# First attention of a hybrid encoder layer: three groups of key blocks per unit, the short rests stacked, ten transposes instead of twelve

## The chip, the cores and the metric

The kernel runs on one core of a Trainium2 chip. TensorE (PE) multiplies matrices and writes to PSUM; VectorE (DVE) and ScalarE (ACT) take results out of PSUM; GpSimd (POOL) works between SBUF tiles; SyncE (SP) issues most transfers. The metric is the time of one execution in device microseconds, as the median of three runs.

## The reference

One layer of an encoder on 2048 tokens of 1024 features: a norm, a projection to queries, keys, values and gates, two attentions, a gated merge, and a feed-forward part of 4096 features. All inputs are float32. The first attention is the one that is changed:

```python
def windowed_gqa(q, k, v, sink):          # 8 query heads, 2 key heads, 64 features each
    def block(i):                         # 128 queries, 384 keys: the block and its two neighbours
        qi = qb[:, i]
        ki = lax.dynamic_slice_in_dim(kp, i * A_BLOCK, 3 * A_BLOCK, axis=1)
        vi = lax.dynamic_slice_in_dim(vp, i * A_BLOCK, 3 * A_BLOCK, axis=1)
        dist = jnp.abs(q_pos[:, None] - k_pos[None, :])
        valid = (dist <= A_WINDOW) & (k_pos[None, :] >= 0) & (k_pos[None, :] < s)
        sc = jnp.einsum('bqkgd,bskd->bkgqs', qi, ki).astype(jnp.float32) * scale
        sc = sc - slopes[:, :, None, None] * dist.astype(jnp.float32)
        sc = jnp.where(valid, sc, -jnp.inf)
        p = jax.nn.softmax(jnp.concatenate([sc, sink_col], axis=-1), axis=-1)[..., :-1]
        return jnp.einsum('bkgqs,bskd->bqkgd', p.astype(v.dtype), vi)
```

A query sees the keys at most 128 tokens away, so of the 384 keys of a block each query uses 257.

## The kernel before, in words

Dense products are made of split operands: a value is written as a rounded high part and a low part (the rest), and products of both are added in PSUM. `hl` tiles hold the two parts of weights, `ph` and `pl` the two parts of attention weights, and a tile of v holds its high part in 64 columns and its low part in 64 more, so that one product with v gives two sums of 64 rows each, which L813 and L814 add.

The work runs in stages: the projections by a fast matrix scheme (`zb`), then the first attention (`attn_a`), the second attention (`attn_b`), the merge, and the feed-forward part (`b`). While the attentions run, pieces of the remaining projections are put in as filler (`mm`, lines 203 to 205); `paced` holds each piece back until the attention unit of a given number has issued its last product.

A unit of the first attention is one key head g and one block i of 128 queries with its four query heads; there are 32 units, 28 with three blocks of keys and four (i = 0 and i = 15, for each g) with two. Inside a unit the queries are arranged as four sub-blocks u of 32 queries by four heads, so that each u has 128 rows, and sub-block u needs only the 288 keys from 32u to 32u + 287 of the 384. In order:

- L770 to L774: q is loaded (`qraw`, SP) and brought into the order of sub-blocks on POOL (`qa`).
- L784, L786: for each u, two products give the scores of 288 keys (PE), and DVE adds the bias and takes the maximum into `s`, a tile of 128 rows by 4 by 384.
- L788 to L793: ACT makes the exponentials and their sums, DVE the reciprocal `ri`.
- L795: POOL multiplies each u by its reciprocal, the shares.
- L802 to L808, for each block c of 128 keys: four transposes into a PSUM bank `pt`, ACT copies it to `ph`, DVE makes `pl`, and two products of 512 columns with v add to `po` (`av`).
- L813, L814: the two halves of `po` are added into `ya`, which SP stores.

Columns of `s` outside a sub-block's 288 keys are zero from the start (L753), so they add nothing to the product.

`drive` starts a unit (up to the shares) two units ahead of the one whose transposes and products are being issued. The order of instructions on each engine is not written out: a planner simulates the program with its own durations and orders each engine's queue by that; the chip then keeps each queue in order. Tiles are taken from pools that grow from the left and the right end of SBUF; a tile that lies where another one lay waits for the last use of that one. The left pools of the first attention are, in order, ka1, va1, qraw, qa, sta, sa, ya, ph, pl, biasa1 and byhead; the second attention's pools (masks, kb0, qb0, braw0, biass0, stb, biass1, qb1, ...) come from the right while the first attention's last units still run. The second attention's biases (`biass0`, `biass1`, `biasl`) are built on POOL at L915, its scores are products at L947 with maxima at L952, its shares are made at L963, its transposes at L975, its splits at L980 and L981, its products at L987.

Of the kernel before, what the change touches and what calls it, by code (L numbers as in the profile page):

```python
# [22 lines left out]
P = 128  # L23
# [72 lines left out]
def encoder_layer(ctx, tc, x, norm_mix, w_in, b_gate, sink, rpb, w_pa, w_pb, w_out,  # L96
# [12 lines left out]
    def pools(stack, side, tags, name):  # L109

        return {t: pool(f"{name}_{t}", side=side, stack=stack) for t in tags}
# [9 lines left out]
    def psum(tag, bufs):  # L121
        n_ps[0] += 1
        return pps[tag].tile([P, 512], F32, tag=tag, bufs=bufs, name=f"{tag}_{n_ps[0]}")
# [549 lines left out]
    s_a = ExitStack()  # L673
    ap_ = pools(s_a, "left", ("ka1", "va1", "qraw", "qa", "sta", "sa", "ya", "ph", "pl", "biasa1", "byhead"), "a")
    ap_.update(pools(s_a, "right", ("biasa0", "va0", "ka0"), "a"))
# [79 lines left out]
    def load_kv(g, m, behind=None):  # L755
        k, kd = kas[g][:, :, m * (S // 2) : (m + 1) * (S // 2)], ks_a[m][g]
        with tc.issue_after(behind) if behind else nullcontext():
# [3 lines left out]
            SY.dma_start(vas[g][:, 8 * m : 8 * m + 8].bitcast(F32), vs_a[m][g])  # L761

    def attn_a(g, i):
        c0, c1 = (1 if i == 0 else 0), (2 if i == 15 else 3)
# [8 lines left out]
        began.append(SY.dma_start(by_head, qs_a[g][i // 8][:, :, i % 8]).ins)  # L773
        G.tensor_copy(out=q.rearrange("p u h q -> p h u q"), in_=by_head.rearrange("p h (u q) -> p h u q", u=4))  # L774
        ka, v = kas[g], vas[g]
        st = T(ap_, [P, 8, 4], F32, "sta", 8)
# [15 lines left out]
        V.tensor_tensor(out=sm, in0=sm, in1=es, op=ALU.add)  # L792
        V.reciprocal(ri, sm)  # L793
        for u, (lo, hi) in enumerate(span):
            share = G.tensor_scalar(s[:, u, lo:hi], s[:, u, lo:hi], ri[:, u : u + 1], 1.0, ALU.mult, ALU.mult)  # L795
        shares.append(share.ins)
        yield
        po = psum("av", 1)
        for c in range(c0, c1):
            pt = psum("pt", 2)  # L800
            for u in range(4):
                PE.transpose(pt[:, u * P : (u + 1) * P], s[:, u, c * P : (c + 1) * P], ident)  # L802
            ph = T(ap_, [P, 512], F32R, "ph", 3)
            pl = T(ap_, [P, 512], F32R, "pl", 3)
            A.copy(ph, pt)
            V.tensor_tensor(out=pl, in0=pt, in1=ph.bitcast(F32), op=ALU.subtract)
            PE.matmul(po, v[:, i - 1 + c, :], ph, start=c == c0, stop=False)
            last = PE.matmul(po, v[:, i - 1 + c, :], pl, start=False, stop=c == c1 - 1).ins  # L808
        done.append(last)
# [846 lines left out]
```

## Time and profile before

| | |
|---|---|
| Time, median of 3 runs (lowest to highest) | 2607.2 us (2606.03 to 2607.28) |
| The profiled execution | 2605.6 us, span 2603.8 us |
| PE, weight loads, DVE, ACT, POOL busy | 2571.4, 2143.3, 1608.0, 1232.4, 368.1 us |
| Instructions | 34627 |

All times of the profile are from the start of the span of the profiled execution. A row of a group of instructions reads: line of the kernel, engine, operation, output from inputs by the names of the tiles, shapes as partitions by elements, count, busy time in us, mean ns of one, and the idle time of the engine just before them with what ended it. A row of the timeline reads: start, length, engine, line, operation and tiles, count of merged instructions, and in brackets the idle time before it. `PEld` is the loading of weights into TensorE, which overlaps its products. The ends of products are modelled; their starts are not.

### The profile page before, as it was taken

To read this page: it belongs to the slowest core of one execution; us is meant where nothing else is said; L and a number is where in the kernel's file an instruction comes from. 1 tells how busy PE (TensorE), PEld (TensorE's weight loads), DVE (VectorE), ACT (ScalarE), POOL (GpSimd) and SP (SyncE) were. 2 spreads that over 40 slices of the span, in tenths; PEclk is the share of its full clock that TensorE was granted. 3 is DMA by queue.
4 is the path that set the end of the run, shared out by engine and by line. 5 is a ranking of instruction groups with operands and counts; after the bars stand their busy time and mean duration, and the time that the engine had idled before them with its cause. 6 is when DMAs were issued, how large, how long until landed. Compare 5 with 4: busy or idle time off the path is not lost.

```text
span 2603.8 us, 34627 instructions
## 1 busy us (share of the span) xinstructions
PE 2571.4 (99%) x12140; PEld 2143.3 (82%) x12140; DVE 1608.0 (62%) x2621; ACT 1232.4 (47%) x2261; POOL 368.1 (14%) x493
## 2 busy tenths in 40 slices
PE   8999999999999999999999999999999999999999
PEld 6888788788888888888888888888888888888887
DVE  8865666665544444665478677766656535554766
ACT  5334356666555555542335544644444322323454
POOL 1000124444655541000000000100000000000010
PEclk9999999999999999999999999999999999999999
DMA  5657486465975745865466665854428825445555
GB/s 185 203 155 202 132 260 166 119 167 154 247 212 173 207 140 188 273 202 161 143 198 207 238 222 200 306 173 146 158 100 313 290 97 186 146 148 167 186 193 171
DMA packets 354127, 490.40 MB, mean 188 GB/s; under 512 B 28808, under 2 KB 188808, under 8 KB 351776
## 3 DMA queue, kind: packets, MB, share of 16 engines
q1 hardware_dynamic: 346896, 471.14, 57.6%
q10 hardware_dynamic: 7056, 17.04, 1.8%
q8 instruction: 96, 1.57, 0.2%
q14 instruction: 79, 0.65, 0.1%
HBM read 328.64 MB, written 159.45 MB: 187 GB/s over the span
## 4 chain that ended last, share of the span: by engine, by line
PE 90%; DVE 4%; DMA 2%; ACT 2%; issue 1%; SPq 0%; POOL 0%; DVEq 0%; POOLq 0%; ACTq 0%
PE b L300 15%; PE b L302 15%; PE b L301 15%; PE mm L203 6%; PE mm L205 6%; PE mm L204 6%; PE zb L300 3%; PE zb L302 3%; PE zb L301 3%; PE pt L203 2%; PE pt L204 2%; PE pt L205 2%; PE av L987 2%; PE pt L975 2%; PE s L947 2%; PE pt L802 1%
## 5 line engine op out<-in xcount | busy, mean ns | idle before, releaser
L301 PE MATMUL b<-dwh,dah 128*128 128x512 f32 x896 | 348.5, 389 | 0.0
L302 PE MATMUL b<-dwh,dah 128*128 128x512 f32 x896 | 347.6, 389 | 0.0
L300 PE MATMUL b<-dwh,dah 128*128 128x512 f32 x896 | 339.6, 389 | 0.0
L296 ACT CAST dah<-da 128x1024 fp32r<-128x1024 f32 (+1 forms) x128 | 120.9, 945 | 368.0 <-PE b L302 245.9
L297 DVE TENSOR_TENSOR dah<-da,dah 128x1024 fp32r<-128x1024 f32 (+1 forms) x128 | 139.5, 1090 | 221.3 <-ACT dah L296 216.8
L301 PE MATMUL b<-ubh,uwhlb 128*128 128x512 f32 x592 | 230.3, 389 | 0.0
L300 PE MATMUL b<-ubh,uwhlb 128*128 128x512 f32 x592 | 230.2, 389 | 0.0
L302 PE MATMUL b<-ubh,uwhlb 128*128 128x512 f32 x592 | 229.2, 389 | 0.0
L203 PE MATMUL mm<-hT,whl 128*128 128x512 f32 x544 | 218.6, 402 | 0.0
L205 PE MATMUL mm<-hT,whl 128*128 128x512 f32 x544 | 215.2, 396 | 0.0
L204 PE MATMUL mm<-hT,whl 128*128 128x512 f32 x544 | 214.4, 394 | 0.0
L301 PEld LDWEIGHTS b<-dwh,dah 128*128 128x128 f32 x896 | 168.2, 188 | 35.0
L302 PEld LDWEIGHTS b<-dwh,dah 128*128 128x128 f32 x896 | 168.2, 188 | 34.9
L300 PEld LDWEIGHTS b<-dwh,dah 128*128 128x128 f32 x896 | 168.2, 188 | 34.9
L300 PE MATMUL zb<-zh,zwhl 128*128 128x512 f32 x476 | 186.7, 394 | 8.3 <-DVE zc L293 3.5
L301 PE MATMUL zb<-zh,zwhl 128*128 128x512 f32 x476 | 186.5, 392 | 0.0
L302 PE MATMUL zb<-zh,zwhl 128*128 128x512 f32 x476 | 183.5, 392 | 0.3 <-DVE zwhl L297 0.3
L293 DVE TENSOR_TENSOR uc<-b,uc 128x512 f32<-128x512 f32 x160 | 109.1, 689 | 105.0 <-PE b L302 104.0
L1526 POOL TENSOR_TENSOR st<-st,power 128x1 f32<-128x1 f32 x16 | 13.4, 841 | 925.2 <-DVE st L1525 925.2
L300 PEld LDWEIGHTS b<-ubh,uwhlb 128*128 128x128 f32 x592 | 111.1, 188 | 23.4 <-issue 0.4
L301 PEld LDWEIGHTS b<-ubh,uwhlb 128*128 128x128 f32 x592 | 111.1, 188 | 23.2
L302 PEld LDWEIGHTS b<-ubh,uwhlb 128*128 128x128 f32 x592 | 111.1, 188 | 23.1
(254 smaller groups left out, 5839.3 us busy)
## 6 DMA issues: line engine op xcount, KB each, us to landing
at<-uc SPq DMA_DIRECT2D x224, 256.0 KB
da<-at SPq DMA_DIRECT2D x96, 512.0 KB
dw<-in_w_down_dram SPq DMA_DIRECT2D x160, 256.0 KB
uraw<-in_w_up_dram SPq DMA_DIRECT2D x32, 1024.0 KB
raw<-in_w_in_dram SPq DMA_DIRECT2D x34, 512.0 KB
zraw<-in_w_in_dram SPq DMA_DIRECT2D x16, 1024.0 KB
z<-zg SPq DMA_DIRECT2D x64, 256.0 KB
qraw<-qs_a SPq DMA_DIRECT2D x32, 256.0 KB
```

The costliest lines, as they stand in the source:

```text
L203: PE.matmul(ps, lh, rh, start=first, stop=False)
L204: PE.matmul(ps, lh, rl, start=False, stop=False)
L205: PE.matmul(ps, ll, rh, start=False, stop=last)
L293: return eng.tensor_tensor(out=out, in0=a, in1=b, op=op).ins
L296: A.copy(hi, src)
L297: return eng.tensor_tensor(out=lo, in0=src, in1=hi.bitcast(F32), op=ALU.subtract).ins
L300: PE.matmul(ps, lh, rh, start=first, stop=False, skip_group_check=True)
L301: PE.matmul(ps, lh, rl, start=False, stop=False, skip_group_check=True)
L302: PE.matmul(ps, ll, rh, start=False, stop=last, skip_group_check=True)
L947: PE.matmul(ps[:, :n], q[:, i, :], kv[:, z, B_R0[i] // 4 : (B_R0[i] + B_NR[i]) // 4, 4 * B_C0[j] : 4 * (B_C0[j] + w)], start=z == 0, stop= ...
L975: PE.transpose(pt[:kp, at + (i - i0) * P : at + (i - i0 + 1) * P], s[i][:, rr : rr + kp], ident)
L987: last = PE.matmul(po[:, i0 * P : (i0 + ni) * P], v[:kp, c, :], src[:kp, o : o + ni * P], start=first, stop=(c == 7 and z == 1), skip_grou ...
```

## The change

A unit's transposes, splits and products are put in three groups instead of one per block of keys.

- The first group is block 1, which all four sub-blocks use in full: four transposes, `ph` and `pl`, two products of 512 columns.
- The second is block 0 for u = 0 and 1 and block 2 for u = 2 and 3: four transposes into one bank, one `ph` and one `pl`, and for each of the two blocks two products of 256 columns.
- The third holds the rests: block 2 for u = 0 and 1 (32 and 64 keys) and block 0 for u = 2 and 3 (64 and 32 keys). The rest of u = 1 is put beside that of u = 0, in columns 320 to 383 of u = 0, and that of u = 3 beside that of u = 2, in columns 32 to 63 of u = 2. So one transpose brings two rests, and two transposes do for the group. In `ph` the high part of each rest takes 64 rows and its low part the other 64, written by DVE to the other half of the partitions; one product of 256 columns for each block, with a tile `ve` that holds the 64 rows of v twice, gives both.

DVE writes the moved rests scaled by the reciprocal; POOL's shares leave those columns out. The doubled rows of v are copied on POOL, four copies of 64 rows by 128 columns per unit (two in an edge unit), into a new pool `ve` of three buffers of 1 KB, at the end of the left pools. All products of a unit are listed in `todo` and issued behind its transposes and splits. An inner unit has 10 transposes, two products of 512 columns and six of 256; an edge unit 7, two and three.

```diff
--- before.py
+++ after.py
@@ -671,7 +671,7 @@
     s_h = ExitStack()
     hpl = [pool(f"hT{n}", side="left", stack=s_h) for n in range(4)]
     s_a = ExitStack()
-    ap_ = pools(s_a, "left", ("ka1", "va1", "qraw", "qa", "sta", "sa", "ya", "ph", "pl", "biasa1", "byhead"), "a")
+    ap_ = pools(s_a, "left", ("ka1", "va1", "qraw", "qa", "sta", "sa", "ya", "ph", "pl", "biasa1", "byhead", "ve"), "a")
     ap_.update(pools(s_a, "right", ("biasa0", "va0", "ka0"), "a"))
     hp = {}
 
@@ -760,6 +760,9 @@
             SY.dma_start(k[64:128, 1].bitcast(F32), kd[0:64])
             SY.dma_start(vas[g][:, 8 * m : 8 * m + 8].bitcast(F32), vs_a[m][g])
 
+    def v_rows(g, k, c):
+        return vas[g][64 - 32 * c : 128 - 32 * c, k]
+
     def attn_a(g, i):
         c0, c1 = (1 if i == 0 else 0), (2 if i == 15 else 3)
         if bias_a[g] is None:
@@ -772,6 +775,12 @@
         s = sas[len(began) % 4]
         began.append(SY.dma_start(by_head, qs_a[g][i // 8][:, :, i % 8]).ins)
         G.tensor_copy(out=q.rearrange("p u h q -> p h u q"), in_=by_head.rearrange("p h (u q) -> p h u q", u=4))
+        ve = T(ap_, [P, 2, P], F32R, "ve", 3)
+        for c in (0, 2):
+            if c0 <= c < c1:
+                rows = v_rows(g, i - 1 + c, c)
+                for half in (slice(0, 64), slice(64, P)):
+                    G.tensor_copy(out=ve[half, c // 2], in_=rows)
         ka, v = kas[g], vas[g]
         st = T(ap_, [P, 8, 4], F32, "sta", 8)
         mx, nm, sm, es, ri = (st[:, k, :] for k in range(5))
@@ -791,21 +800,53 @@
             A.activation(s[:, u, lo:hi], s[:, u, lo:hi], AF.Exp, bias=nm[:, u : u + 1], accum_out=sm[:, u : u + 1])
         V.tensor_tensor(out=sm, in0=sm, in1=es, op=ALU.add)
         V.reciprocal(ri, sm)
+        for u, lo, hi, at in ((1, 2 * P, span[1][1], s[:, 0, 320:384]), (3, span[3][0], P, s[:, 2, 32:64])):
+            if lo < hi:
+                V.tensor_scalar(at, s[:, u, lo:hi], ri[:, u : u + 1], 1.0, ALU.mult, ALU.mult)
         for u, (lo, hi) in enumerate(span):
+            lo, hi = max(lo, P if u == 3 else 0), min(hi, 2 * P if u == 1 else hi)
             share = G.tensor_scalar(s[:, u, lo:hi], s[:, u, lo:hi], ri[:, u : u + 1], 1.0, ALU.mult, ALU.mult)
         shares.append(share.ins)
         yield
         po = psum("av", 1)
-        for c in range(c0, c1):
+        todo = []
+
+        def whole(keys):
             pt = psum("pt", 2)
-            for u in range(4):
+            for u, c in keys:
                 PE.transpose(pt[:, u * P : (u + 1) * P], s[:, u, c * P : (c + 1) * P], ident)
+            at = slice(keys[0][0] * P, (keys[-1][0] + 1) * P)
             ph = T(ap_, [P, 512], F32R, "ph", 3)
             pl = T(ap_, [P, 512], F32R, "pl", 3)
-            A.copy(ph, pt)
-            V.tensor_tensor(out=pl, in0=pt, in1=ph.bitcast(F32), op=ALU.subtract)
-            PE.matmul(po, v[:, i - 1 + c, :], ph, start=c == c0, stop=False)
-            last = PE.matmul(po, v[:, i - 1 + c, :], pl, start=False, stop=c == c1 - 1).ins
+            A.copy(ph[:, at], pt[:, at])
+            V.tensor_tensor(out=pl[:, at], in0=pt[:, at], in1=ph[:, at].bitcast(F32), op=ALU.subtract)
+            for c in sorted({c for _, c in keys}):
+                us = [u for u, cc in keys if cc == c]
+                cs = slice(us[0] * P, (us[-1] + 1) * P)
+                todo.extend((v[:, i - 1 + c, :], t[:, cs], cs) for t in (ph, pl))
+
+        def halved(cs):
+            pt = psum("pt", 2)
+            ph = T(ap_, [P, 512], F32R, "ph", 3)
+            for c in cs:
+                u, k = (0, 2 * P) if c == 2 else (2, 0)
+                PE.transpose(pt[:, u * 64 : u * 64 + P], s[:, u, k : k + P], ident)
+            a = slice(0 if 2 in cs else 1, 2 if 0 in cs else 1)
+            by_u = ph.rearrange("p (u q) -> p u q", u=4)
+            src = pt[:, 0 : 2 * P].rearrange("p (a q) -> p a q", a=2)[:, a]
+            for us, here, there in ((by_u[:, 0::3][:, a], slice(0, 64), slice(64, P)),
+                                    (by_u[:, 1:3][:, a], slice(64, P), slice(0, 64))):
+                A.copy(us[here], src[here])
+                V.tensor_tensor(out=us[there], in0=src[here], in1=us[here].bitcast(F32), op=ALU.subtract)
+            for c in cs:
+                at = slice(0, 256) if c == 2 else slice(256, 512)
+                todo.append((ve[:, c // 2], ph[:, at], at))
+
+        whole([(u, 1) for u in range(4)])
+        whole([(u, 2 * (u // 2)) for u in range(4) if c0 <= 2 * (u // 2) < c1])
+        halved([c for c in (2, 0) if c0 <= c < c1])
+        for n, (rows, p, at) in enumerate(todo):
+            last = PE.matmul(po[:, at], rows, p, start=n == 0, stop=n == len(todo) - 1, skip_group_check=True).ins
         done.append(last)
         t = T(ap_, [64, 512], F32, "ya", 2)
         t4 = t.rearrange("d (h u q) -> d h u q", h=4, u=4)
```

## The prediction

> **What bounds the kernel now.** I read the page first (engine shares, then the chain that ended last), then one stretch of the trace, that of the first attention, by busy time, by groups of instructions, by the chain and instruction by instruction.
>
> ```profile
> PE 2571.4 (99%) x12140; PEld 2143.3 (82%) x12140; DVE 1608.0 (62%) x2621; ACT 1232.4 (47%) x2261; POOL 368.1 (14%) x493
> PE 90%; DVE 4%; DMA 2%; ACT 2%; issue 1%; SPq 0%; POOL 0%; DVEq 0%; POOLq 0%; ACTq 0%
> ```
>
> TensorE carries the kernel: 99% busy, 90% of the chain. A busy PE is not PE at its peak, so what counts is how often it starts an instruction. The first attention runs from 372 to 646 us. Two rows of busy time by stretch (columns: window, length, then busy us of PE, weight loads, DVE, ACT, POOL with counts), and the chain of that stretch by line:
>
> ```profile
> 372.00:646.00 274.00, 268.21 (x1451) 223.50 (x1450) 169.97 (x487) 182.56 (x507) 126.91 (x192) 1.00 0.58 159
> 450.00:500.00 50.00, 47.28 (x260) 39.20 (x258) 31.10 (x88) 32.22 (x90) 20.04 (x32) 1.00 0.49 125
> ```
>
> ```profile
> by line: PE mm L203 17.0%; PE mm L204 16.8%; PE mm L205 16.8%; PE pt L802 11.8%; PE s L784 8.1%; PE av L808 7.2%; PE av L807 6.2%; ACT sa L791 4.4%; DVE pl L806 2.1%; issue 1.8%; ACT ph L805 1.6%; DVE sa L786 1.2%; PE s L947 0.9%; ACT ya L8
> ```
>
> PE is idle for 274.0 - 268.2 = 5.8 us of the stage, at full clock (1.00). Half the chain is dense filler (mm); attention's transposes (pt) and value products (av) are 25%. Some 11% of it, 30 us, is ACT, DVE and issue (4.4 + 2.1 + 1.8 + 1.6 + 1.2): there PE work is not what sets the end.
>
> **The change, part by part.** The groups that it touches, in that stretch:
>
> ```profile
> L806 DVE TENSOR_TENSOR pl<-pt,ph 128x512 fp32r<-128x512 f32 x92 | 62.8, 688 | 18.4 <-ACT ph L805 17.9
> L802 PE MATMUL pt<-ident,sa 128*128 128x128 f32 x368 | 55.9, 272 | 2.5 <-DVE pl L806 2.3 <-DVE sta L793 0.2
> L795 POOL TENSOR_SCALAR sa<-sa,sta 128x288 f32<-128x288 f32 x112 | 54.5, 506 | 51.0 <-DVE sta L793 40.8 <-ACT ph L805 4.4 <-ACT ya L813 2.9
> L805 ACT CAST ph<-pt 128x512 fp32r<-128x512 f32 x92 | 53.1, 585 | 51.6 <-PE pt L802 50.8
> L808 PE MATMUL av<-pl,va 128*128 128x512 f32 x92 | 38.0, 413 | 1.8 <-DVE pl L806 1.4
> ```
>
> 92 groups of four transposes are 28 inner units of three key blocks and 4 edge units (i = 0 or 15) of two. Their pace on PE, from the starts:
>
> ```profile
> 430.26 0.40 PE L203 MATMUL mm<-hT,whl 128*128 128x512 f32 x1
> 430.49 0.60 PE L802 MATMUL pt<-ident,sa 128*128 128x128 f32 x4
> 430.85 0.48 PE L204 MATMUL mm<-hT,whl 128*128 128x512 f32 x1
> 431.16 0.40 PE L205 MATMUL mm<-hT,whl 128*128 128x512 f32 x1
> ```
>
> A product of 512 columns takes 430.49 - 430.26 = 0.23 us; four transposes take 431.16 - 430.49 less one such product, 0.44, so 0.11 each. Products of 256 columns with a full weight tile run in the second attention:
>
> ```profile
> 721.68 0.27 PE L987 MATMUL av<-phb,vb 128*128 128x256 f32 x1
> ...
> 722.03 0.28 PE L987 MATMUL av<-plb,vb 128*128 128x256 f32 x1
> ```
>
> Two more stand between these: (722.03 - 721.68) / 3 is 0.12 us from start to start, so halves pay almost nothing extra.
>
> PE. An inner unit goes from 12 transposes to 10 (-0.22 us) and from six products of 512 columns (1.38) to two of 512 and six of 256 (0.46 + 0.72 = 1.18; -0.20): -0.42, times 28 is -11.8. An edge unit goes from 8 transposes and four products (0.88 + 0.92) to 7, two of 512 and three of 256 (0.77 + 0.46 + 0.36): -0.21, times 4 is -0.8. Together -12.6 us. The products now stand behind all of a unit's transposes in program order; the first two could start up to 0.66 us (six transposes) later. I cost that at nothing: filler stands between groups, as in the rows at 430 us, and without it the waits of PE for ACT and DVE, below, would grow.
>
> ACT and DVE, evictions. The rest group is copied and subtracted in two halves of 64 rows by 256 columns each, results of the subtraction 64 partitions away. Rows of the same form by width, and one of 64 rows:
>
> ```profile
> L981 DVE TENSOR_TENSOR plb<-pt,phb 128x512 fp32r<-128x512 f32 x32 | 21.6, 688 | 3.5 <-ACT phb L980 3.2
> L981 DVE TENSOR_TENSOR plb<-pt,phb 128x384 fp32r<-128x384 f32 x32 | 17.4, 553 | 10.1 <-ACT phb L980 10.1
> L980 ACT CAST phb<-pt 128x512 fp32r<-128x512 f32 x32 | 18.4, 588 | 16.1 <-PE pt L975 15.7
> L980 ACT CAST phb<-pt 128x384 fp32r<-128x384 f32 x32 | 15.0, 478 | 21.4 <-PE pt L975 21.4
> L814 DVE TENSOR_TENSOR ya<-av,ya 64x512 f32<-64x512 f32 x32 | 21.8, 680 | 8.6 <-ACT ya L813 8.4
> ```
>
> Width counts and rows do not (680 against 688 ns). Extended to 256 columns, a copy takes 0.588 - 2 x 0.110 = 0.37 and a subtraction 0.688 - 2 x 0.135 = 0.42. A unit's third group then costs ACT 0.74 instead of 0.59 and DVE 0.84 instead of 0.69: +0.15 each. No row shows a write to other partitions; between 0.34 (half of the 512 row) and 0.69 (all of it) I take 0.42.
>
> DVE, two small scaled copies per unit (64 and 32 columns) behind the reciprocal. Nearest rows:
>
> ```profile
> 376.20 0.38 DVE L792 TENSOR_TENSOR sta<-sta 128x4 f32<-128x4 f32 x1 [1.17 <-ACT sa L791]
> 376.61 0.18 DVE L793 RECIPROCAL sta<-sta 128x4 f32<-128x4 f32 x1
> ```
>
> ```profile
> 374.15 2.40 POOL L180 TENSOR_TENSOR whl<-raw,whl 128x1024 fp32r<-128x1024 f32 x1 [0.74 <-ACT whl L179]
> ```
>
> I take 0.2 each, like the reciprocal; above, one could be held by a POOL instruction, as the first row seems to be: it ends at 376.58, just behind POOL's 376.55. A hold lasts at most one share of 0.506, so 0.2 to 0.7. DVE's sum is +0.55 us a unit, 18 over the stage, beside 104 us in which it is idle; ACT's is +5 beside 91. Both are hidden except where PE already waits for them.
>
> POOL. Each of the four (edge: two) doubled v copies lies between the two copies below, nearer the first:
>
> ```profile
> L735 POOL COPY byhead<-sink_t 32x2 f32<-32x2 f32 x4 | 0.7, 179 | 0.1
> L774 POOL CAST qa<-qraw 128x512 fp32r<-128x512 f32 x30 | 18.4, 615 | 52.0 <-issue 40.0 <-PE s L784 5.2 <-DMA qs_b<-z 3.0
> ```
>
> At (0.615 - 0.179) / 510 = 0.85 ns a column, 128 columns take 0.29; 120 copies make 35 us, while the shares lose 96 of their columns (-0.08 a unit). POOL rises from 127 to some 159 of 274 us: hidden, unless a copy stands ahead of a share that PE needs (a rival). The copies wait for nothing but the v load. No DMA is added.
>
> Where PE waits for ACT and DVE. The largest gap, and a chain of the same sort at 554 us:
>
> ```profile
> 488.74 0.66 PE L802 MATMUL pt<-ident,sa 128*128 128x128 f32 x4 [2.02 <-DVE pl L806]
> ```
>
> ```profile
> 555.33 0.59 ACT ph L805
> 555.92 1.56 ACT sa L791 x6
> 557.48 0.48 ACT z L425
> ...
> 557.98 0.69 DVE z L426
> ...
> 558.75 0.59 DVE pl L806
> ...
> 559.39 0.50 PE av L808
> ```
>
> Such stretches come about every 33 us, seven in the stage: ACT copies, exponentials and subtractions in turn while the filler is out. PE work saved inside them gains nothing: 11% of 12.6 is +1.4. And each holds one or two evictions and perhaps the small copies: 0 to 1.0 us longer (two halves at +0.15 on both engines, +0.4 of small copies), 0 to +7; I take +3.
>
> The start of the second attention. The new ve buffers lie on top of the left stack, behind byhead, which ends at byte 145,504; they reach to 148,576. The second attention's biass1 (146,368 to 150,464) lay on free memory and now shares it with them, and qb1 with the first of them. So the bias and q of its second unit must wait for the first attention's last ve products.
>
> ```profile
> 574.08 3.05 POOL L915 TENSOR_TENSOR biass<-braw,masks 128x288 f32<-128x288 f32 x3 [3.46 <-DMA qraw<-qs_a]
> ```
>
> ```profile
> 619.38 1.04 PE L947 MATMUL s<-kb,qb 128*128 128x288 f32 x6
> ...
> 623.18 0.78 PE L947 MATMUL s<-kb,qb 128*128 128x384 f32 x4
> ...
> 645.23 0.39 PE L807 MATMUL av<-ph,va 128*128 128x512 f32 x1
> ...
> 664.66 0.40 PE L947 MATMUL s<-kb,qb 128*128 128x288 f32 x1 [0.79 <-DMA kb<-ks_b]
> ```
>
> Biases could be built from 574 us and the second unit's scores ran between 619 and 624; now the build (3.05) comes after about 646. Queued behind it on POOL are the splits of the filler's weights, and behind qb1's load on SP the filler's own loads. Cover: filler and the first unit's own work, which keep PE going until the wait at 664.66. Bounds: -0.8, if the 0.79 us wait for kb1 goes because the first attention ends earlier, and +6, the build and as much again for scores and maxima with no filler left. I take +1.5.
>
> Sum: -12.6 + 1.4 + 3 + 1.5 = -6.7 us. The profiled execution has a span of 2603.8 and a time of 2605.6, 1.6 under the median of 2607.2; moved to the median, 2607.2 - 6.7 = 2600.5.
>
> **The rivals.**
>
> Eaten by ACT and DVE (no change): the seven stretches lengthen by their full +7 and PE's 12.6 falls mostly before them, where PE then only waits longer. With the second attention's bound (-12.6 + 1.4 + 7 + 3) the time is 2606. For it: ACT is busy 67% of the stage and its exponentials stand ahead of the copies in its queue. Against: 89% of the chain is not theirs. Part of it is the hold between DVE and POOL: both small copies held by a share, +1.0 in each stretch. [...]
>
> POOL's queue (slower): in an inner unit the 1.16 us of v copies stands ahead of its shares, while the filler is out. Each such unit costs 1.16 and saves 0.42. If all 28 do, 2600.5 + 28 x 1.16 = 2633; from 11 units on it ends above 2612.4, slower. Against it: the share row shows POOL idle 40.8 us waiting for DVE's reciprocal, time in which copies fit.
>
> The second unit's late start (slower): its lead, from scores at 619 to shares done at 633, is lost, and filler runs out before it: 14 us instead of 1.5, 2613. For it, that lead exists today; against it, only two of 32 units have it, and it must be lost nearly whole (13.4 us) before the sign turns.
>
> ```profile
> 630.90 2.14 POOL L963 TENSOR_SCALAR sb<-sb,stb 128x288 f32<-128x288 f32 x4
> ```
>
> It doesn't do what it says: if a product of 256 columns paid for its whole weight load instead of 0.12 us, av would rise to 0.46 + 6 x 0.19 = 1.60 a unit, the transposes' saving would be gone and 2607.2 + 3 + 1.5 = 2611.7 would stand. The rows at 721 us speak against it; loads overlap products there.
>
> ```profile
> L808 PEld LDWEIGHTS av<-pl,va 128*128 128x128 f32 x92 | 17.3, 188 | 7.2 <-DVE pl L806 5.1
> ```
>
> **How the numbers follow.** Sum as worked out: 0.48 (faster). Eaten: 0.24, weight loads: 0.03 (no change). POOL's queue: 0.17, late start: 0.08 (slower). A measurement here tells 0.2% (5.2 us) from no change: faster 0.48, same 0.27, slower 0.25. The likeliest case's own range has its bounds at 2607.2 - 13.4 - 1.2 (the spread of the runs) = 2592.6, with nothing given back, and 2602. The range adds the eaten case (to 2612), 2613 of the late start, and POOL's queue up to 13 units: 2592 to 2616, which leaves out some 0.15.
>
> **What would show it.** Right: transposes fall from 368 to 308; av products of 256 columns start 0.12 us apart; the stage, 372 to 646, ends about 8 us sooner; copies of 64x256 near 0.37 and 0.42 us; PE idle in the stage 6 to 10 us. Wrong: idle of PE behind DVE's subtractions or POOL's shares above 12 us; PE idle between 630 and 670 us waiting for biass1 or qb1; small DVE copies of 0.5 us; 256-column products 0.19 us apart.

## The result, and the profile after

The changed kernel takes 2638.7 us (median; 2635.9 to 2644.7) against 2607.2 for the kernel before: ratio 1.0122, 95% interval 1.0109 to 1.0134, some 31.5 us slower where 6.7 faster was forecast. Its profiled execution took 2639.7 us with a span of 2637.8, against 2603.8. Of these 34.0 us, 2.9 lie ahead of the stage, in work that both kernels share (the first scores of the first attention start at 366.81 instead of 363.91 us).

The work itself is what was forecast. Groups of instructions of the kernel after, 372 to 664 us, in the columns known from before:

```profile
L840 DVE TENSOR_TENSOR ph<-pt,ph 64x256 fp32r<-64x256 f32 x55 | 23.2, 422 | 11.9 <-ACT ph L839 10.6
L839 ACT CAST ph<-pt 64x256 fp32r<-64x256 f32 x55 | 20.2, 367 | 39.3 <-PE pt L833 32.9 <-DVE ph L840 5.7
L783 POOL CAST ve<-va 64x128 fp32r<-64x128 f32 x110 | 32.1, 292 | 39.8 <-PE av L849 31.4 <-PE pt L817 4.0
L849 PE MATMUL av<-ph,ve 128*128 128x256 f32 x57 | 13.8, 321 | 8.8 <-DVE ph L840 8.7
L805 DVE TENSOR_SCALAR sa<-sa,sta 128x64 f32<-128x64 f32 x30 | 8.6, 285 | 0.8
```

The halved copies take 0.367 us and the subtractions 0.422 (forecast 0.37 and 0.42), the copies of v 0.292 (0.29), the small copies 0.285 (0.2 to 0.7). Writing 64 partitions away shows no cost above 0.015 us: subtractions of 128x256 that stay on their own partitions take 0.407 in the same window (L822, of edge units), and 0.417 in the kernel of a later experiment (one eviction of the third group). What changed is behind the second bar of each row: DVE, ACT, POOL and PE wait for one another. Busy time by stretch (window, length, busy us of PE, weight loads, DVE, ACT, POOL, granted clock, DMA share, GB/s), first of the kernel before:

```profile
380.00:640.00 260.00, 254.21 (x1383) 211.88 (x1381) 162.17 (x463) 176.08 (x490) 119.19 (x184) 1.00 0.56 153
```

and of the kernel after:

```profile
380.00:640.00 260.00, 234.39 (x1242) 196.31 (x1241) 169.77 (x524) 165.05 (x484) 132.96 (x271) 0.94 0.52 140
390.00:400.00 10.00, 7.38 (x31) 6.13 (x30) 8.68 (x33) 9.68 (x34) 8.96 (x21) 0.66 0.75 213
600.00:610.00 10.00, 7.24 (x32) 5.88 (x31) 7.53 (x21) 7.85 (x25) 7.69 (x13) 0.71 0.53 148
```

PE starts 1242 instructions in these 260 us instead of 1383. It is idle for 25.6 us instead of 5.8, and its granted clock falls from 1.00 to 0.94: in the worst stretches of 10 us it starts some 31 instructions, where the kernel before starts 53 on average. What PE waited for there, in the kernel after (us in all, times, longest), and the chain of its stage:

```profile
PE av L849 <- DVE ph L840: 8.7, 7, 2.3
PE pt L817 <- DVE pl L822: 7.8, 6, 2.5
PE s L793 <- DVE sta L795: 4.4, 8, 0.8
```

```profile
by line: PE mm L203 15.5%; PE mm L204 15.3%; PE mm L205 15.3%; ACT sa L800 9.9%; PE av L849 8.2%; PE pt L817 5.7%; PE s L793 5.6%; DVE sa L795 3.9%; issue 3.2%; PE pt L833 1.6%; ACT ph L821 1.4%; DVE ph L840 1.3%; DMA biasa<-in_dist_a_dram 
```

ACT's exponentials (L800) have gone from 4.4% of the chain to 9.9%. Why they stand in it is seen in one unit, in the timeline of the kernel after:

```profile
461.69 0.38 PE L833 MATMUL pt<-ident,sa 128*128 128x128 f32 x2
...
462.39 0.36 ACT L839 CAST ph<-pt 64x256 fp32r<-64x256 f32 x1
...
463.31 0.52 ACT L800 ACTIVATE sa<-sa,sta 128x288 f32<-128x288 f32 x1
463.61 0.42 DVE L840 TENSOR_TENSOR ph<-pt,ph 64x256 fp32r<-64x256 f32 x1
...
465.34 0.52 ACT L800 ACTIVATE sa<-sa,sta 128x288 f32<-128x288 f32 x1
465.69 0.66 PE L817 MATMUL pt<-ident,sa 128*128 128x128 f32 x4 [1.45 <-DVE pl L822]
465.98 0.37 ACT L839 CAST ph<-pt 64x256 fp32r<-64x256 f32 x1
...
466.86 0.42 DVE L840 TENSOR_TENSOR ph<-pt,ph 64x256 fp32r<-64x256 f32 x1
```

The two transposes are done at 462.1. Their split is complete at 467.28, over five us later, with work of 1.57 us. The four steps are written as copy, subtraction, copy, subtraction, all into one tile `ph`, and the second copy waits for the first subtraction (the 5.7 us behind DVE in its row above). They write the same 64 rows but different columns: the subtraction those of u = 0 and 3, the copy those of u = 1 and 2, which lie between them. So the third group crosses from ACT to DVE, back to ACT and back to DVE, and at each crossing it stands in a queue behind other work: here DVE's scores and ACT's four exponentials. PE's gap of 1.45 us in this stretch ends with another subtraction (L822, of the next unit), which stands in the same two queues.

To compare stretches of kernels that do different work, I price PE's instructions at their pace at full clock (0.227 us for 512 columns, as seven steps between such products from 362.73 to 364.32 us of the kernel after give it, and in proportion for fewer columns, an estimate that puts 256 columns at 0.114, where starts lie 0.12 apart; 0.11 for a transpose) and count as lost what the time has above that, idle time and lowered clock together. Each stretch's figure is its length minus the priced work that starts in it:

| lost, us | 380–640 | 640–720 | 340–1040 |
|---|---|---|---|
| before | 17.7 | 3.5 | 34.8 |
| after | 55.8 | 7.2 | 79.4 |

By these prices the change saves 13.4 us of work (the forecast, with 0.12 us for a product of 256 columns, had 12.6). The difference of the last column, 44.6, less 13.4 is 31.2, and the two profiled executions differ by 34.0 - 2.9 = 31.1 behind the work ahead of the stage. The loss is in the first attention: 38.1 us more from 380 to 640 us, of which PE's idle time is 25.6 - 5.8 = 19.8. The 80 us behind 640 add 3.7 us; in the kernel after they still hold the end of the first attention, whose last product with v starts at 678.49 us instead of 645.91.

### The profile page after: what moved, and what is told of

It reads as the page before. It is cut to its first block, busy times and chain, and to the rows that moved or that the text cites. A ratio compares the mean times of both kernels' runs of the same rounds, so it can differ in the third digit from the quotient of the medians.

```text
span 2637.8 us, 34887 instructions
## 1 busy us (share of the span) xinstructions
PE 2580.9 (98%) x12140; PEld 2151.1 (82%) x12140; DVE 1630.0 (62%) x2717; ACT 1240.6 (47%) x2297; POOL 401.1 (15%) x613
## 3 DMA queue, kind: packets, MB, share of 16 engines
q8 instruction: 96, 1.57, 0.2%
## 4 chain that ended last, share of the span: by engine, by line
PE 88%; DVE 5%; ACT 3%; DMA 2%; issue 1%; SPq 1%; POOL 1%; DVEq 0%; POOLq 0%; ACTq 0%
PE b L300 15%; PE b L302 15%; PE b L301 15%; PE mm L203 6%; PE mm L205 6%; PE mm L204 6%; PE zb L300 3%; PE zb L302 3%; PE zb L301 3%; PE pt L203 2%; PE pt L204 2%; PE pt L205 2%; PE av L1028 2%; PE pt L1016 2%; PE s L988 2%
## 5 line engine op out<-in xcount | busy, mean ns | idle before, releaser
L300 PEld LDWEIGHTS b<-dwh,dah 128*128 128x128 f32 x896 | 168.2, 188 | 34.8
L1567 POOL TENSOR_TENSOR st<-st,power 128x1 f32<-128x1 f32 x16 | 13.4, 843 | 925.1 <-DVE st L1566 925.1
```

Of the source, the lines that this page charges most:

```text
L300: PE.matmul(ps, lh, rh, start=first, stop=False, skip_group_check=True)
```

## The experiments

**Is it the order of the third group's evictions?** The theory: the serial split makes most of the loss. The rivals: POOL's copies of v, and the products put off behind all groups.

```diff
-            for us, here, there in (...):
+            for us, here, there in both:
                 A.copy(us[here], src[here])
+            for us, here, there in both:
                 V.tensor_tensor(out=us[there], in0=src[here], ...)
```

> The changed kernel with one edit: in the third group both ACT copies stand ahead of both DVE subtractions, so the second copy no longer waits for the first subtraction. Serial-split theory (the chain ACT, DVE, ACT, DVE of the third group is what PE waits for in the stretches without filler): PE's wait behind the third group's subtraction falls from 19.7 to under 6 us, the clock stays at 1.00 and the time falls from 2638.7 to 2612 to 2620. POOL-queue theory and deferred-products theory: the time stays within 4 us of 2638.7, because ACT's copy would only wait for something else.

Measured: 2625.7 us, ratio 1.0067 [1.0050, 1.0084], some 14 us less than the changed kernel by the ratios (13.0 by the bare times; the kernel before, run beside it, took 2608.0). That is more than the 4 us of the rivals, but it misses the theory's 2612 to 2620, and the clock is 0.97, not 1.00. The 19.7 us of the expectation are the waits of products (8.7) and of their weight loads (11.0) together; they overlap, and products alone are compared here. Of the kernel with the copies first, a row of its timeline, the window of the stage, and the group of products that read the third group's result:

```profile
461.18 0.75 ACT L840 CAST ph<-pt 64x256 fp32r<-64x256 f32 x2
```

```profile
380.00:640.00 260.00, 244.32 (x1335) 207.27 (x1334) 176.10 (x546) 176.23 (x508) 139.34 (x283) 0.97 0.55 149
```

```profile
L851 PE MATMUL av<-ph,ve 128*128 128x256 f32 x60 | 14.0, 311 | 5.2 <-ACT ph L821 3.2 <-ACT sa L800 1.1 <-DVE ph L842 0.9
```

The two copies now run back to back, the wait of PE for the subtraction falls from 8.7 to 0.9 us, ACT's exponentials fall from 10.6% to 1.8% of the chain from 372 to 646 us, and the lost time of the stage from 55.8 to 38.4. The order of two pairs of instructions is nearly half of the 31.5 us. The other half stays open.

**POOL's copies of v.**

```diff
-        ve = T(ap_, [P, 2, P], F32R, "ve", 3)
-        ... four G.tensor_copy(out=ve[half, c // 2], in_=rows)
-                todo.append((ve[:, c // 2], ph[:, at], at))
+                todo.append((v[:, i - 1 + c, :], ph[:, at], at))
```

> The changed kernel without the doubled rows: no POOL copies, no ve tile, and the third group's products take the block's v tile as weights instead (this leaves the right values out of the rests; PE's instructions stay the same in number and size). POOL-queue theory (copies, and their wait for the products of three units ago, delay shares and q behind them in POOL's queue): 2612 to 2620. Late-start theory (ve lies over biass1 and qb1): 3 to 6 us faster than 2638.7, all of it after 640 us of the span. Serial-split theory: idle of PE in the stage stays above 18 us and the time above 2630.

Measured: 2631.7 us, 1.0096 [1.0076, 1.0117], about 7 us less. But the stage loses the same (55.2 instead of 55.8), and PE still waits 9.8 us for the subtractions. The gain is elsewhere: of the 7.7 us between the two profiled executions, some 3 lie behind 640 us and 3 ahead of 340 us, in work that both kernels share. So POOL's queue did not carry the loss in the stage.

**The products behind their groups.**

```diff
         whole([(u, 1) for u in range(4)])
+        products()
         whole([...])
+        products()
         halved([...])
-        for n, (rows, p, at) in enumerate(todo): ...
+        last = products(True)
```

> The changed kernel with the products issued right behind each group's split in program order, not behind all three groups. Deferred-products theory (ph and pl tiles, the transposes' banks and the av bank are held too long): PE's wait of transposes behind the subtraction falls from 17 us to under 8 and the time is 2620 to 2626. Serial-split theory: the third group still ends last, 2632 to 2640. POOL-queue theory: no difference.

Measured: 2636.2 us, 1.0108 [1.0093, 1.0123]: its interval overlaps that of the changed kernel. The counterpart puts the products of the kernel before behind all of a unit's groups:

> The kernel before with one edit: a unit's six products stand behind its three groups of transposes and splits. Deferred-products theory: 2612 to 2618, with PE waiting for av or transposes longer. If the deferral costs no more than in the run by group (2.5 us): 2607 to 2611.

Measured: 2606.7 us, 0.9994 [0.9984, 1.0003]. In the kernel before, deferral costs nothing that shows. Both edits together, copies first and products by group, with POOL's copies of v kept:

> The changed kernel with two edits together: both ACT copies of the third group ahead of both DVE subtractions, and a group's products right behind the group. POOL's copies of v stay. If the gains of the two edits add up (13 and 2.5 us): 2623. If the order of the copies already brings all that the order of the products can bring: 2625.5. If POOL's copies hold more once the rest is out of the way: 2626 to 2628; the same two edits without POOL's copies gave 2619.5.

Measured: 2625.5 us, 1.0067 [1.0052, 1.0082], the same as with the copies first alone. Beside the run with products by group alone (2636.2) it is a second test of the order of the copies: 10.7 us less.

**POOL's copies in the kernel before**, read by nothing:

```diff
         G.tensor_copy(out=q.rearrange("p u h q -> p h u q"), ...)
+        ve = T(ap_, [P, 2, P], F32R, "ve", 3)
+        ... four G.tensor_copy(out=ve[half, c // 2], in_=rows)
```

> The kernel before with only the doubled v copies added on POOL, into ve tiles that nothing reads (extra work, the result does not use it). POOL-queue theory in its plain form (1.16 us of copies a unit ahead of shares): 2615 to 2625. If only the copies' wait for old products matters, that wait isn't here and the time is 2607 to 2610. Serial-split and deferred-products theories: 2606 to 2611, the upper end if biass1 lying under ve costs something.

Measured: 2622.8 us, 1.0058 [1.0043, 1.0073], which seems to speak for POOL's queue. The timeline of this kernel shows where:

```profile
379.84 0.62 POOL L780 CAST ve<-va 64x128 fp32r<-64x128 f32 x2 [5.71 <-DMA va<-vs_a]
...
385.66 0.61 POOL L774 CAST qa<-qraw 128x512 fp32r<-128x512 f32 x1
386.32 0.98 PEld L790 LDWEIGHTS s<-ka,qa 128*128 128x128 f32 x4 [6.39 <-POOL qa L774]
386.32 1.09 PE L790 MATMUL s<-ka,qa 128*128 128x288 f32 x3 [6.16 <-POOL qa L774]
```

A copy waits 5.71 us for the first load of v, q stands behind it on POOL, and PE waits 6.16 us for q. This kernel loses 34.5 us in the stage, 16.9 more than the kernel before. Of these, 9.5 lie from 380 to 400 us, around this one event; the other 7.4 are spread over the rest of the stage, and no run says what they are. In the kernel after, PE's waits for POOL are small (1.6 us for qa in the stage), and without the copies its stage loses the same. So the run shows what such a queue can cost, not what it cost there.

**Taking parts away one after another.** Copies first, products by group and no doubled v:

> The changed kernel with three things at once: both copies of the third group ahead of its subtractions, products behind each group, and no doubled rows (the third group's products take the block's v tile, so the rests get wrong values; PE's instructions stay). The order that the planner makes is another one each time. Theory that the delays add: 2638.7 - 13 - 7 - 2.5 = 2616. Theory that the split chain was the whole of it and each single run still paid another stall: 2596 to 2604, the PE sum. Theory that the stage is now paced by ACT and DVE whatever the chain: above 2620, PE idle from 380 to 640 us still above 12 us.

Measured: 2619.5 us, 1.0043 [1.0028, 1.0058], with 17.4 us of PE idle in the stage: between the first theory and the third. Beside the run that keeps the copies of v (2625.5) the stage loses about the same (35.7 against 36.9 us); the difference is the start of the second attention, 7.6 against 12.3 us. Kernel with both mended orders and the copies of v kept, its waits and one window there:

```profile
PE s L1001 <- DMA qb<-qs_b: 3.6, 1, 3.6
PE pt L1029 <- POOL sb L1017: 1.5, 1, 1.5
```

```profile
680.00:690.00 10.00, 4.89 (x21) 3.99 (x19) 3.00 (x10) 5.33 (x18) 6.55 (x7) 0.65 1.08 258
```

This is the late start of the second attention: SP's load of q (L988 of this kernel) waits 3.8 us for products of the first attention, and PE's wait of 3.6 us for q is 0.3 in the run without `ve`. That run still loses 7.6 us from 640 to 720, against 3.5 in the kernel before, so `ve` explains about 5 of the 9 us. In the changed kernel itself the stretch loses 7.2 us, and 6.2 without `ve`: there most of the 3.7 us is not the shared memory's.

Next, without the small copies on DVE too:

```diff
-        for u, lo, hi, at in (...):
-            if lo < hi:
-                V.tensor_scalar(at, s[:, u, lo:hi], ri[:, u : u + 1], 1.0, ALU.mult, ALU.mult)
```

> The run before this one, and DVE's two small scaled copies a unit left out as well (the rests of u = 1 and 3 are then missing from the result). If they matter (0.28 us each, 15 us of DVE over the stage, right behind the reciprocal and ahead of scores' maxima and subtractions): 4 to 10 us below the run with all three. If they are hidden: within 3 us of it.

Measured: 2615.3 us, 1.0028 [1.0017, 1.0039]. About 4 us less, which the first theory named; but the two intervals overlap, and the stage's loss did not fall with it (38.7), so it is not shown to be the copies'.

And with the third group of inner units evicted in one copy and one subtraction:

```diff
+            if len(cs) == 2:
+                pl = T(ap_, [P, 512], F32R, "pl", 3)
+                A.copy(ph[:, 0:256], pt[:, 0:256])
+                V.tensor_tensor(out=pl[:, 0:256], in0=pt[:, 0:256], in1=ph[:, 0:256]..., op=ALU.subtract)
+                todo.append((v[:, i + 1, :], ph[:, 0:256], slice(0, 256)))
+                todo.append((v[:, i - 1, :], pl[:, 0:256], slice(256, 512)))
+                return
```

> The stripped kernel (copies first, products by group, no doubled v, no small copies; 2615.3) with the third group of the 28 inner units evicted by one copy and one subtraction of 128x256 instead of two copies and two subtractions of 64x256; its two products read one the high part and one the low part, so the rests come out wrong, and PE's work stays the same. Theory A (the two extra evictions of a unit, +0.37 us on ACT and +0.42 on DVE, are what remains of the loss): 2603 to 2607, with PE idle below 12 us from 380 to 640 us. Theory B (the grouping, with block 0 and block 2 mixed in one group, and the order that the planner makes of it): 2612 to 2616, idle still about 17.

Measured: 2611.7 us, 1.0012 [1.0003, 1.0021], between the two theories, at the edge of the second, with 12.7 us of PE idle. Some 4 us point to the extra evictions (the stage's loss falls from 38.7 to 32.8, though the intervals of the two times overlap), and the time is still 3 to 4 us above the kernel before, with 13.4 us less work for PE.

**The other direction: PE's work alone taken out of the kernel before.** Three transposes for the outer blocks, products of 384 columns for them, evictions of the same size (0.587 us a copy and 0.689 a subtraction in the trace); the blocks are also taken in the order 1, 0, 2:

```diff
-        for c in range(c0, c1):
+        for c in (1, 0, 2):
+            us = {0: range(3), 1: range(4), 2: range(1, 4)}[c]
+            cs = slice(us[0] * P, (us[-1] + 1) * P)
...
-            PE.matmul(po, v[:, i - 1 + c, :], ph, ...)
+            PE.matmul(po[:, cs], v[:, i - 1 + c, :], ph[:, cs], ...)
```

> The kernel before with PE work alone taken away, about as much as the change takes: in an inner unit the transpose of u = 3 in block 0 and of u = 0 in block 2 are left out (10 remain) and those blocks' products run over 384 columns, 512 columns less a unit; copies and subtractions stay at 512 columns each (they read some columns twice, so the result is wrong). Nothing is added on any other engine. Theory that PE carries the stage, as the forecast's sum had it: 2594 to 2598. Theory that the stretches without filler are paced by ACT and DVE and eat what PE saves: 2604 to 2610, PE idle from 380 to 640 us rising from 5.8 to 12 or more.

Measured: 2603.4 us, 0.9989 [0.9980, 0.9998]. By the prices above, 13.4 us of work are taken from a TensorE that is 99% busy, just what the change takes; about 3 arrive (0.5 to 5.2 by the interval). The time is just under the second theory's range. Window of this kernel:

```profile
380.00:640.00 260.00, 249.47 (x1344) 208.96 (x1343) 162.86 (x469) 175.40 (x491) 123.03 (x189) 1.00 0.59 158
```

PE is idle for 10.5 us instead of 5.8, and the stage loses 26.8 instead of 17.7: 9 of the 13 us are given back, with the clock still at 1.00. Of these 9, 4.7 show as idle time of PE; the rest are products that start later while PE counts as busy. In the chain from 372 to 646 us the filler and the first attention's work on PE hold 74.3%, against 83.9% in the kernel before: other engines have taken over what PE gave up.

Splitting the last block's eviction in two in the kernel before, without and with this removal of PE work:

```diff
+            parts = (slice(0, 256), slice(256, 512)) if c == c1 - 1 else (slice(0, 512),)
+            for cs in parts:
+                A.copy(ph[:, cs], pt[:, cs])
+            for cs in parts:
+                V.tensor_tensor(out=pl[:, cs], in0=pt[:, cs], in1=ph[:, cs]..., op=ALU.subtract)
```

> The kernel before, with the copy and the subtraction of each unit's last block cut into two column halves of 128x256, copies first; PE's work is unchanged. Theory A (extra evictions cost time although ACT and DVE are idle for a third of the stage or more): 2612 to 2617, PE idle above 10 us from 380 to 640. Theory B (what remains of the loss comes from grouping and order): within 2 us of the kernel before, since +0.15 us per unit on ACT and DVE is small beside their idle time.

> The kernel before with PE's work alone taken away (two transposes and 512 columns of products per inner unit, wrong result; 2603.4) and the evictions of block 2 cut into two halves as well (of 256 columns each, copies first). Theory A: 2609 to 2615, so that split evictions turn the small gain into a loss. Theory B: 2602 to 2605.

Measured: 2612.3 us, 1.0018 [1.0009, 1.0028], and 2603.0 us, 0.9983 [0.9974, 0.9993]. The split costs 5 us in the one (with some 7 us of PE idle, not the 10 that theory A named) and nothing that shows in the other. It is a cost of a few us at most, and not the whole remainder; what it hangs on, perhaps on where the planner puts the instructions, no run shows.

**Ways to a faster kernel.** The doubled v loaded by SP instead of copied by POOL (with two buffers of `ve` and `pl` and both mended orders), and the same with the pools in another order, so that `qb1` shares no space with `ve`:

```diff
-                    G.tensor_copy(out=ve[half, c // 2], in_=rows)
+                    SY.dma_start(ve[half, c // 2].bitcast(F32), vs_a[k // 8][g][64 - 32 * c : 128 - 32 * c, k % 8])
```

```diff
-"sa", "ya", "ph", "pl", "biasa1", "byhead", "ve")
+"sa", "ya", "ph", "ve", "pl", "biasa1", "byhead")
```

> A full version: copies ahead of subtractions, products behind each group, the doubled rows loaded by SP from DRAM (two transfers a block) in place of POOL's copies, two ve and two pl buffers so that ve ends where the pools of before ended and biass1 lies free again. POOL-queue and late-start theories: as the run with all three, within 5 us. If SP's queue is delayed by the 120 extra issues (0.57 us each): 5 to 15 us above it. Below 2607 it would beat the kernel before.

> The same version without the extra filler. Against the run with loaded doubled rows (2619) only the place of ve differs: if qb1's wait for ve cost the 8 us lost near 690 us there, 2609 to 2613; if it was the extra transfers in SP's queue, 2617 to 2621.

Measured: 2619.0 us, 1.0046 [1.0029, 1.0062], and 2620.2 us, 1.0052 [1.0037, 1.0067]. The other order halves the loss from 640 to 720 us (13.0 to 6.0), but the time does not fall: it stays in the second theory's range, though that SP's queue is the reason is not shown.

More filler under the first attention, four of the second attention's pieces moved forward, in the kernel before and in the last version:

```diff
-    paced(fill, range(12), 24, 3)
+    paced(fill, range(14), 28, 3)
...
-    paced(fill, range(20, 44), 38, 4)
+    paced(fill, range(20, 40), 38, 4)
```

> The kernel before with more filler under the first attention: 28 pieces in place of 24, taken from those behind the second attention. If PE's idle there comes from filler running out: idle from 380 to 640 us under 4 us and the time 2600 to 2606. If not: 2606 to 2612.

> The full version with loaded doubled rows, its ve pool put ahead of pl so that qb1 lies over no ve buffer, and with the 28 pieces of filler. If the change's saving was lost because filler runs out and PE idles, it now shows: PE idle from 380 to 640 us under 8 us, clock 1.00, 2594 to 2602, below the kernel before with the same filler. If ACT and DVE pace the stage whatever the filler: 2610 to 2618.

Measured: 2616.5 us, 1.0038 [1.0024, 1.0052], above both ranges, and 2617.4 us, 1.0047 [1.0032, 1.0062], in the second range. The end of the second attention in the kernel before (first row), and in it with the moved filler (second):

```profile
1000.00:1060.00 60.00, 59.55 (x288) 49.74 (x287) 39.01 (x51) 34.61 (x50) 2.29 (x1) 1.00 0.74 248
```

```profile
1000.00:1060.00 60.00, 52.63 (x257) 43.05 (x257) 34.92 (x53) 37.88 (x63) 2.12 (x4) 0.94 0.69 221
```

In the last version the stage's loss falls from 35.5 to 26.2 us, so filler does cover the waits; but the second attention ends without it and there loses as much again. Cover was moved, not made. No version that computes the whole result was faster than the kernel before beyond what the measurement tells.

## Why the prediction was wrong, point by point

The runs, put in order, with the loss from 380 to 640 us beside each:

| kernel | ratio | lost in the stage, us |
|---|---|---|
| after | 1.0122 | 55.8 |
| copies first | 1.0067 | 38.4 |
| and products by group | 1.0067 | 36.9 |
| and no doubled v | 1.0043 | 35.7 |
| and no small copies | 1.0028 | 38.7 |
| and one eviction of the third group | 1.0012 | 32.8 |
| before, PE's work alone removed | 0.9989 | 26.8 |
| before | 1 | 17.7 |

- **"An inner unit goes from 12 transposes to 10 ... Together -12.6 us"** was right as work: transposes are 248 + 60 = 308, the work priced above falls by 13.4 us, and four products of 256 columns in the kernel after start at 462.38, 462.50, 462.62 and 462.74, 0.12 us apart.
- **"PE work saved inside them gains nothing: 11% of 12.6 is +1.4"** was the first failed step. The run with PE's work alone removed takes 13.4 us away and saves 2.9, so some 10 are lost, not 1.4; the run that splits an eviction besides agrees (2603.0 us). The share of the chain that ACT and DVE held belongs to a schedule with PE's full work. With PE shorter, the others take over in stretches that the chain had counted as PE's (PE's 83.9% of it become 74.3%). This is the mechanism of the rival "Eaten by ACT and DVE"; its "PE's 12.6 falls mostly before them" was the better account. Its time, 2606, was not: most of the loss is in the next point.
- **"0 to 1.0 us longer ..., 0 to +7; I take +3"** for the evictions was the largest failure. It added up durations (+0.15 on ACT and on DVE) and never followed the order in which they are issued: copy, subtraction, copy, subtraction into one tile, in two queues. That order alone costs about 14 us by the run with the copies first, and 11 by the pair with products by group. The extra instructions without that order point to about 4 (the table's step to one eviction; 5 in the kernel before, nothing that shows in the kernel with less PE work).
- **The clock** was taken as full throughout. In the kernel after it is 0.94 over the stage. If PE could have used all of that time, 0.06 x 260 is 16 us of the loss: an estimate from above, worked out from the window's clock, since it overlaps with waits.
- **"I cost that at nothing"**, of the products behind all transposes, was right in the kernel before (0.9994); in the changed kernel the intervals (1.0108 and 1.0122) don't tell the two apart.
- **"The copies wait for nothing but the v load"** was wrong: they wait 31.4 us for older products that read the same buffers of `ve`. In the stage it cost little: without the copies the stage loses the same (55.2 against 55.8, 35.7 against 36.9). Without copies and `ve` the time falls by 7 and 6 us all the same, in large part outside the stage. The rival "POOL's queue", which would have given a time near the one measured, is not what happened.
- **"I take +1.5"** for the start of the second attention was too low: 3.7 us in the kernel after, and some 9 (12.3 against 3.5) in the version with both mended orders. The cause named, memory shared between `ve` and the second attention's tiles, is shown for some 5 of the 9 and for 1 of the 3.7; the rest is open. In the rival of the late start, 13.4 us is where the time would have measured as slower; the sign of the sum turns at 12.6 - 1.4 - 3 = 8.2.
- **The small copies**, 0.2 forecast and up to 0.7 if held, took 0.285 and 0.272 us. The forecast allowed for a hold by one of POOL's shares. The row that it took for a hold, 0.38 us, is the longest of 32 of its line in the kernel before, whose median is 0.162. Of 60 copies in the kernel after the median is 0.254 us and the longest 0.531, and these two, 0.41 us together, run while POOL is in its shares:

```profile
466.57 1.91 POOL L808 TENSOR_SCALAR sa<-sa,sta 128x288 f32<-128x288 f32 x4 [4.54 <-DVE sta L802]
```

```profile
467.32 0.41 DVE L805 TENSOR_SCALAR sa<-sa,sta 128x64 f32<-128x64 f32 x2
```

POOL's shares of 288 columns take 0.513 us on average, against 0.506 before. The longest pair of copies, 0.83 us from 623.56, ends beside POOL's shares (624.39 and 624.36 us). A hold of both copies in each stretch, which the rival names, is not shown, and what lengthened the long ones is open.
- **The stage end**, forecast some 8 us sooner, and idle of 6 to 10 us were wrong: the last product with v starts 32.6 us later, and idle is 25.6 us from 380 to 640. PE's waits for L840 and L822 there, 8.7 + 7.8 + 1.1 (the last before L833), are 17.6, above the 12 us named as what would show the sum wrong.

What stays open: between the kernel with one eviction of the third group (1.0012) and the kernel with PE's work alone removed (0.9989) lie 6 us of stage loss. They differ in grouping, in the widths evicted and in the whole order that the planner makes of it, and no run separates these. By the intervals each step of the table is known to some 3 to 6 us, and each edit lets the planner arrange all queues anew, so steps of 4 us are indications. Firm are the step of 14 us for the order of the copies and the small gain of the run with PE's work alone removed. Each loss is read from one profiled execution.

## What to carry to other kernels

When a result is split in pieces by two engines in turn, first issue all pieces of the one, then all of the other: here the ordering between writes to different parts of a tile made over five us of 1.57 us of work in the unit at 462 us, and some 14 us in the time of the run. (Tiles of their own for the pieces were not tried.) That PE was 99% busy said little about what removing its work gains (13.4 us taken away, about 3 gained); take the work away alone, leaving part of the computation out, before building what makes the removal possible, and forecast with the gain that arrives. Filler moved under one stage was missing in another here (PE busy for 52.63 instead of 59.55 of 60 us), so see both ends before moving it.

## What was unexpected in the hardware

TensorE's granted clock fell to 0.50 around a gap of 2.52 us. Timeline and windows of the kernel after:

```profile
393.25 1.12 PE L817 MATMUL pt<-ident,sa 128*128 128x128 f32 x4 [2.52 <-DVE pl L822]
...
398.83 0.41 PE L849 MATMUL av<-ph,va 128*128 128x256 f32 x1
399.05 0.42 PE L849 MATMUL av<-pl,va 128*128 128x256 f32 x1
399.26 0.36 PE L849 MATMUL av<-ph,va 128*128 128x256 f32 x1
```

```profile
390.00:392.00 2.00, 0.73 (x5) 0.36 (x3) 1.90 (x9) 2.00 (x10) 1.60 (x4) 1.00 1.16 346
392.00:394.00 2.00, 0.75 (x4) 0.75 (x5) 1.45 (x5) 1.95 (x7) 2.00 (x5) 0.65 0.97 208
394.00:396.00 2.00, 2.00 (x9) 1.63 (x8) 1.69 (x8) 1.95 (x6) 1.85 (x6) 0.50 0.98 348
396.00:398.00 2.00, 2.00 (x11) 1.87 (x10) 1.97 (x6) 1.98 (x9) 1.89 (x5) 0.50 0.23 75
398.00:400.00 2.00, 1.91 (x8) 1.52 (x8) 1.67 (x8) 1.80 (x6) 1.61 (x5) 0.64 0.42 86
400.00:402.00 2.00, 2.00 (x13) 1.75 (x14) 1.97 (x7) 1.18 (x2) 1.89 (x5) 1.00 0.39 110
```

The clock drops to half although PE works on for about 6 us of it, and products of 256 columns start 0.21 to 0.22 us apart instead of 0.12. By the windows 0.35 x 2 + 0.50 x 4 + 0.36 x 2 = 3.4 us of full pace are gone, some of it in the gap itself. The length of one gap does not decide between the cases seen here. In the kernel before, one gap of 2.02 us (at 488.74) left the clock at 1.00 in its 50 us window. In the kernel with the copies first, three gaps of 0.87, 0.51 and 0.89 us end at 389.76, 391.06 and 392.55, and the clock drops among them:

```profile
388.00:390.00 2.00, 1.13 (x8) 0.79 (x8) 1.92 (x7) 2.00 (x8) 0.39 (x1) 1.00 1.23 307
390.00:392.00 2.00, 1.16 (x7) 0.61 (x6) 1.87 (x9) 1.93 (x7) 2.00 (x5) 0.84 1.08 315
392.00:394.00 2.00, 1.45 (x5) 1.30 (x6) 2.00 (x6) 2.00 (x8) 1.72 (x6) 0.50 0.99 302
```

What decides between these cases is not shown here.
